# A trunk layer's opening: one block of modulation sums ahead of the first products, and K stretches in halves of the column sets

## The chip, the cores and the metric

The kernel runs on one core of one Trainium2 chip. The metric is the device time of a whole execution in microseconds (us). Five engines are named as the profile names them: PE (TensorE) multiplies, PEld loads its weights, DVE (VectorE) and ACT (ScalarE) work on tiles in on-chip memory, POOL does little here, and SP issues the transfers (DMA) from the chip's main memory. Each engine takes its instructions in the order in which they stand in its queue.

## What is computed

One decoder layer on 256 tokens of width 2048: a SwiGLU feed-forward, a mixer (pooling and windowed attention), a second feed-forward. Each is preceded by a norm and a modulation whose shift and scale come from a product of silu(c) with a 2048 x 18432 matrix, w_ada. Only the first feed-forward's start is touched:

```
mod = (silu(c) @ w_ada + b_ada).reshape(B, 9, 1, D)
h = modulate(rms_norm(x, g_ffn1), mod[:, 0], mod[:, 1])     # h * (1 + scale) + shift
x = x + 0.5 * mod[:, 2] * swiglu(h, w_ffn1_gu, w_ffn1_down) # (silu(h @ gate) * (h @ up)) @ down
```

All is float32. A product of activations and weights is made of three products of rounded halves: hi*hi, lo*hi and hi*lo.

## The kernel before

The 2048 channels are 16 ktiles of 128, and the 256 tokens two token tiles. Weight columns are taken in sets of 1024 (`Set`). For each pair of ktiles of a set, one transfer of 1 MB brings the weights (L169, tile `raw`, six buffers). For each ktile ACT casts the high half (`wh`, L180, three buffers), DVE subtracts for the low half (`wl`, L184, three buffers), and PE runs twelve products of 128 x 512 (L194, L196, L198): two token tiles, two halves of the columns, three products each. They add up in four of the eight PSUM banks. The next set takes the other four, which serve small things until then.

The opening is everything up to the end of the first six sets (gate and up columns, alternating). Their products cannot start before x is normed and the first shift and scale are known, and these need 2 x 2048 columns of w_ada, 32 MB. So the columns come in blocks (`ada_block`). A block of 256 channels brings 4 MB, for 16 ktiles of c, in rows of 1 KB; one of 512 channels brings 8 MB in rows of 2 KB. DVE multiplies each ktile's slice by c and adds it to `acc` (L450, L452). In the two 256 blocks every other ktile goes through PE instead, with c as the stationary side (L448). A product with ones sums the partitions (L456). `mod_col` turns that row, which lies alike on all partitions, into a column for each 128 channels: DVE masks with the identity (L103), reduces (L106), and adds bias and gain (L110 to L113). Then `h_mod` modulates the transposed, normed x, and writes the halves `hh` and `hl`.

The order of the work: block 0 (256 channels), then for the first set its first two ktiles, then block 1 (256 channels), and then the rest. All six sets run over four ktiles at a time (n = 0 to 3, 12 pairs of ktiles each). At the end of each such segment four banks are taken out: for n = 0 ACT copies them to on-chip memory (L520), later DVE adds them to what lies there (L522). Under n = 0, 1 and 2 the next 512-channel block is loaded and summed, one eighth (1 MB) with each pair of ktiles, `nxt.pop(0)()`, eight in twelve pairs. A scheduler orders each engine's queue from this text, so that some instructions stand ahead of others that come first in it. Transfers go to one queue, SP's, and take turns on eight completion counters: a transfer that comes eight places later waits at its issue until the earlier one on its counter has landed.

## Time and profile before

| what | value |
|---|---|
| median of three runs | 2041.13 us (2040.59 to 2041.98) |
| profiled execution, from the first instruction to the last | 2041.3 us |
| busy: PE, DVE, ACT | 2008.7, 1472.2, 987.3 us |
| transfers over the span | 523.69 MB, mean 257 GB/s |
| rows of w_ada in 512 KB loads: count, time to landing | 64, 7.5 us |

The page's first part gives busy time, share of the span and instruction count by engine; its groups give the count, the busy time, the mean duration of one in ns, the idle time of the engine before them, and what ended it. A timeline row gives start and duration in us, engine, line, operation, out<-in and count; the duration of a merged row runs from the first start to the last end. A row of windows gives a stretch, its length, the busy time of PE, PEld, DVE, ACT and POOL with their instruction counts, then PE's granted clock, the transfer engines' busy share and GB/s. Engines start an instruction before the one before it has quite ended, so the distance between two starts is shorter than the duration.

### The profile page before, as it was taken

To read this page: it belongs to the slowest core of one execution; us is meant where nothing else is said; L and a number is where in the kernel's file an instruction comes from. 1 tells how busy PE (TensorE), PEld (TensorE's weight loads), DVE (VectorE), ACT (ScalarE), POOL (GpSimd) and SP (SyncE) were. 2 spreads that over 40 slices of the span, in tenths; PEclk is the share of its full clock that TensorE was granted. 3 is DMA by queue.
4 is the path that set the end of the run, shared out by engine and by line. 5 is a ranking of instruction groups with operands and counts; after the bars stand their busy time and mean duration, and the time that the engine had idled before them with its cause. 6 is when DMAs were issued, how large, how long until landed. Compare 5 with 4: busy or idle time off the path is not lost. (4 is left out here: it accounts for less than half of the span.)

```text
span 2041.3 us, 23823 instructions
## 1 busy us (share of the span) xinstructions
PE 2008.7 (98%) x9053; PEld 1648.5 (81%) x9053; DVE 1472.2 (72%) x1698; ACT 987.3 (48%) x1324; POOL 7.3 (0%) x17
## 2 busy tenths in 40 slices
PE   6999999999999999999999999999999999999999
PEld 4788888888788887888788887788888888888887
DVE  5799878788899956777878788755555555566645
ACT  3554454444544546546554455654443444454443
POOL 0000000000000000000000000000000000000000
PEclk9999999999999999999999999999999999999999
DMA  9988758998898855776868887455655656666762
GB/s 337 356 316 301 279 198 305 334 338 313 318 350 334 333 195 183 252 278 229 293 237 288 292 283 270 165 209 207 243 206 206 228 204 214 219 223 231 233 193 69
DMA packets 157915, 523.69 MB, mean 257 GB/s; under 512 B 9353, under 2 KB 23394, under 8 KB 157544
## 3 DMA queue, kind: packets, MB, share of 16 engines
q1 hardware_dynamic: 157800, 522.16, 72.2%
q8 instruction: 71, 1.16, 0.2%
q14 instruction: 44, 0.36, 0.0%
HBM read 520.00 MB, written 2.12 MB: 256 GB/s over the span
## 5 line engine op out<-in xcount | busy, mean ns | idle before, releaser
L180 ACT CAST wh<-raw 128x1024 fp32r<-128x1024 f32 (+2 forms) x731 | 730.9, 1003 | 949.6 <-PE bank L196 874.2
L184 DVE TENSOR_TENSOR wl<-raw,wh 128x1024 fp32r<-128x1024 f32 (+2 forms) x746 | 842.0, 1136 | 452.2 <-ACT wh L180 447.2
L194 PE MATMUL bank<-wh,hh 128*128 128x512 f32 x2072 | 654.5, 390 | 6.7 <-ACT hh L278 5.7
L198 PE MATMUL bank<-wl,hh 128*128 128x512 f32 x2072 | 651.8, 389 | 0.8 <-DVE wl L184 0.5
L196 PE MATMUL bank<-wh,hl 128*128 128x512 f32 x2072 | 652.1, 389 | 0.0
L194 PEld LDWEIGHTS bank<-wh,hh 128*128 128x128 f32 x2072 | 387.1, 188 | 88.4 <-ACT hh L278 7.8
L198 PEld LDWEIGHTS bank<-wl,hh 128*128 128x128 f32 x2072 | 389.0, 188 | 83.4 <-DVE wl L184 3.9
L196 PEld LDWEIGHTS bank<-wh,hl 128*128 128x128 f32 x2072 | 388.7, 188 | 81.5 <-DVE hl L279 1.4
L129 DVE SCALAR_TENSOR_TENSOR acc<-raw,cs,acc 128x1024 f32<-128x1024 f32 x216 | 276.4, 1279 | 41.2 <-DMA raw<-in_w_ada_dram 39.4
L198 PE MATMUL bank<-wl,sh 128*128 128x512 f32 x692 | 216.9, 390 | 1.9 <-DVE wl L184 1.9
L196 PE MATMUL bank<-wh,sl 128*128 128x512 f32 x692 | 216.6, 390 | 0.3 <-DVE sl L298 0.3
L194 PE MATMUL bank<-wh,sh 128*128 128x512 f32 x692 | 216.7, 390 | 0.0
L198 PEld LDWEIGHTS bank<-wl,sh 128*128 128x128 f32 x692 | 129.7, 188 | 29.6 <-DVE wl L184 2.8
L194 PEld LDWEIGHTS bank<-wh,sh 128*128 128x128 f32 x692 | 129.7, 188 | 28.6 <-ACT wh L180 0.6
L196 PEld LDWEIGHTS bank<-wh,sl 128*128 128x128 f32 x692 | 129.8, 188 | 27.9 <-DVE sl L298 1.0
L452 DVE SCALAR_TENSOR_TENSOR acc<-raw,cs,acc 128x1024 f32<-128x1024 f32 (+1 forms) x59 | 68.1, 1154 | 7.0 <-DMA raw<-in_w_ada_dram 6.2
L298 DVE TENSOR_TENSOR sl<-big,sh 128x512 fp32r<-128x512 f32 x88 | 60.0, 683 | 4.2 <-ACT sh L297 4.2
L297 ACT CAST sh<-big 128x512 fp32r<-128x512 f32 x88 | 54.3, 621 | 8.1 <-DVE big L652 8.1
L522 DVE TENSOR_TENSOR big<-bank,big 128x512 f32<-128x512 f32 x60 | 38.1, 682 | 1.2 <-PE bank L198 0.8
L276 ACT ACTIVATE t<-bank,mcol 128x128 f32<-128x128 f32 x90 | 35.0, 463 | 7.8 <-PE bank L264 7.1
L236 ACT ACTIVATE junk<-x_sb 128x512 bf16<-128x512 f32 x24 | 15.1, 629 | 19.9 <-DVE x_sb L322 13.8
L448 PE MATMUL bank<-raw,cs 128*128 128x256 f32 x64 | 19.4, 458 | 3.3 <-DMA raw<-in_w_ada_dram 3.3
(156 smaller groups left out, 698.2 us busy)
## 6 DMA issues: line engine op xcount, KB each, us to landing
raw<-in_w_ffn_gu_dram SPq DMA_DIRECT2D x176, 1024.0 KB, 5.0
raw<-in_w_ada_dram SPq DMA_DIRECT2D x112, 1024.0 KB, 6.4
raw<-in_w_ffn_down_dram SPq DMA_DIRECT2D x88, 1024.0 KB, 5.8
raw<-in_w_in_dram SPq DMA_DIRECT2D x48, 1024.0 KB, 5.0
raw<-in_w_ada_dram SPq DMA_DIRECT2D x64, 512.0 KB, 7.5
raw<-in_w_o_dram SPq DMA_DIRECT2D x16, 1024.0 KB, 7.1
raw<-in_w_pool_up_dram SPq DMA_DIRECT2D x8, 1024.0 KB, 6.9
raw<-in_w_attn_up_dram SPq DMA_DIRECT2D x8, 1024.0 KB, 5.6
```

Of the source, the lines that this page charges most:

```text
L129: nc.vector.scalar_tensor_tensor(out=a[0], in0=raw[:, k, :], scalar=sc, in1=a[0], op0=ALU.mult, op1=ALU.add)
L180: nc.scalar.copy(wh, raw_k)
L184: nc.vector.tensor_tensor(wl[:, e], raw_k[:, e], wh[:, e].bitcast(F32), ALU.subtract)
L194: nc.tensor.matmul(self.banks[t][i], hi[:, sl], wh[:, o], start=first, stop=False)
L196: nc.tensor.matmul(self.banks[t][i], lo[:, sl], wh[:, o], start=False, stop=False)
L198: nc.tensor.matmul(self.banks[t][i], hi[:, sl], wl[:, o], start=False, stop=last)
L276: nc.scalar.activation(h[:, f, :], src, AF.Identity, scale=g_, bias=b_)
L297: nc.scalar.copy(hi, src[:, k:k + n, :])
L298: nc.vector.tensor_tensor(lo, src[:, k:k + n, :], hi.bitcast(F32), ALU.subtract)
L448: nc.tensor.matmul(banks[j], sc.to_broadcast([P, P]), r[:, j, :], start=kk == 0, stop=False)
L452: nc.vector.scalar_tensor_tensor(out=acc[0], in0=r, scalar=sc, in1=acc[0], op0=ALU.mult, op1=ALU.add)
L522: nc.vector.tensor_tensor(a, b, a, ALU.add)
```

## The change

x is loaded first, by token tiles. The first block of w_ada (256 channels) is loaded next, in four pieces, with the gains and biases between the second piece and the third. Its even ktiles go through PE with the weights as the stationary side and c as one moving column, and its sums fall out as columns (`ada_col`); no mask is needed. All other blocks are summed on DVE alone, and end in products with one column of ones. There is no second block ahead of the products: three blocks of 256 channels (two ktiles of h each) and two of 512 (four each) go one piece with each pair of ktiles, from the first pair on (`work`, `tick`). A block's last step (`done`) makes its columns, transposes x and modulates, and stands with the first piece of the next block. Norm, transposes and modulation go by pairs of channel tiles with both token tiles together (`x_T`, `h_pair`).

The sets no longer all run over four ktiles. First all six run over ktiles 0 and 1. Then the sets fall in two groups, sets 0 to 3 and sets 4 and 5: the first runs ktiles 2-3, the second 2-5, the first 4-7, the second 6-11, the first 8-15, the second 12-15. There are 24 segments as before. The first six are copied by ACT, the others added by DVE.

Lines of the changed file are about 7 further on: L187 casts `wh`, L191 makes `wl`, L446 and L448 sum into `acc`, L567 copies, L569 adds, L477 and L542 are the products with one column, L487 and L492 norm and transpose x, L505 makes `hl`.

SP's queue at the start. Names end in buffer numbers; DMAHW0 to DMAHW7 are the eight completion counters. Before:

```order
L461 DMA x_sb<-in_x_dram 128x2x2048
L469 DMA t_3_89<-in_g_ffn_dram 16x128
L469 DMA t_3_89<-in_g_mix_dram 16x128
L469 DMA t_3_89<-in_g_ffn_dram 16x128
L469 DMA t_3_89<-in_pool_scale_dram 8x128
L472 DMA t_4_94<-in_b_ada_dram 32x128 x2
L472 DMA t_4_94<-in_b_ada_dram 32x128 [waits DMAHW0_49]
L440 DMA raw_130<-in_w_ada_dram 128x4x256 [waits DMAHW1_49]
L440 DMA raw_130<-in_w_ada_dram 128x4x256 [waits DMAHW2_49]
```

and now:

```order
L81 DMA x_sb<-in_x_dram 128x2048 x2
L440 DMA raw_90<-in_w_ada_dram 128x4x256 x2
L440 DMA raw_93<-in_w_ada_dram 128x4x256 x2
L512 DMA t_5_96<-in_g_ffn_dram 16x128
L512 DMA t_5_96<-in_g_mix_dram 16x128 [waits DMAHW0_49]
L512 DMA t_5_96<-in_g_ffn_dram 16x128 [waits DMAHW1_49]
L512 DMA t_5_96<-in_pool_scale_dram 8x128 [waits DMAHW2_49]
L515 DMA t_6_101<-in_b_ada_dram 32x128 [waits DMAHW3_49]
L515 DMA t_6_101<-in_b_ada_dram 32x128 [waits DMAHW4_49]
L515 DMA t_6_101<-in_b_ada_dram 32x128 [waits DMAHW5_49]
L440 DMA raw_105<-in_w_ada_dram 128x4x256 [waits DMAHW6_49]
L440 DMA raw_105<-in_w_ada_dram 128x4x256 [waits DMAHW7_49]
```

x and two pieces of the first block now stand ahead of the gains and biases. The third piece (raw_105) waits for counter 6, which is that of the second load of raw_93.

ACT's queue at a segment's end while ACT takes the banks out. Before, from the casts of set 1's last ktiles on:

```order
L180 CAST wh_405<-raw_403 128x1024
L180 CAST wh_421<-raw_403 128x1024
L180 CAST wh_452<-raw_450 128x1024
L520 COPY big_182<-bank_360 128x512
L520 COPY big_182<-bank_361 128x512
L520 COPY big_182<-bank_362 128x512
L520 COPY big_182<-bank_363 128x512
L180 CAST wh_468<-raw_450 128x1024
```

and now, from the first set on:

```order
L187 CAST wh_223<-raw_221 128x1024
L187 CAST wh_239<-raw_221 128x1024
L567 COPY big_215<-bank_217 128x512
L567 COPY big_215<-bank_218 128x512
L187 CAST wh_273<-raw_271 128x1024
L567 COPY big_215<-bank_219 128x512
L567 COPY big_215<-bank_220 128x512
L187 CAST wh_289<-raw_271 128x1024
L567 COPY big_215<-bank_267 128x512
```

In the first list a cast of the next set (wh_452) stands ahead of the four copies. In the second the first cast of the next set (wh_273) stands behind two copies of the banks of the set before (bank_217, bank_218); so it is at the next ends too, up to the fifth.

DVE's queue where it adds the partial sums. Before, one segment of four ktiles under n = 1:

```order
L184 TENSOR_TENSOR wl_879<-raw_860,wh_878 128x1024
L452 SCALAR_TENSOR_TENSOR acc_857<-raw_941,cs,acc_857 128x1024
L184 TENSOR_TENSOR wl_910<-raw_907,wh_909 128x1024
L452 SCALAR_TENSOR_TENSOR acc_857<-raw_941,cs,acc_857 128x1024
L522 TENSOR_TENSOR big_182<-bank_814,big_182 128x512
L522 TENSOR_TENSOR big_182<-bank_815,big_182 128x512
L522 TENSOR_TENSOR big_182<-bank_816,big_182 128x512
L522 TENSOR_TENSOR big_182<-bank_817,big_182 128x512
L184 TENSOR_TENSOR wl_926<-raw_907,wh_925 128x1024
L184 TENSOR_TENSOR wl_949<-raw_946,wh_948 128x1024
L184 TENSOR_TENSOR wl_965<-raw_946,wh_964 128x1024
L452 SCALAR_TENSOR_TENSOR acc_857<-raw_980,cs,acc_857 128x1024 x2
```

and now, the second run over two ktiles (sets 0 and 1):

```order
L448 SCALAR_TENSOR_TENSOR acc_455<-raw_572,cs,acc_455 128x512
L569 TENSOR_TENSOR big_215<-bank_534,big_215 128x512
L448 SCALAR_TENSOR_TENSOR acc_455<-raw_572,cs,acc_455 128x512
L569 TENSOR_TENSOR big_215<-bank_535,big_215 128x512
L448 SCALAR_TENSOR_TENSOR acc_455<-raw_572,cs,acc_455 128x512
L569 TENSOR_TENSOR big_215<-bank_536,big_215 128x512
L569 TENSOR_TENSOR big_215<-bank_537,big_215 128x512
L191 TENSOR_TENSOR wl_590<-raw_587,wh_589 128x1024
L191 TENSOR_TENSOR wl_606<-raw_587,wh_605 128x1024
L448 SCALAR_TENSOR_TENSOR acc_455<-raw_621,cs,acc_455 128x512 x2
L569 TENSOR_TENSOR big_215<-bank_583,big_215 128x512
L448 SCALAR_TENSOR_TENSOR acc_455<-raw_621,cs,acc_455 128x512
```

Before, four low halves (wl) and three sums (acc) stand near four additions (big<-bank). Now there are two low halves and up to four narrower sums to each four additions, and the two low halves of the next segment (wl_590, wl_606) stand behind all four additions of this one.

The diff, with removed lines (they are in the kernel printed above) cut to "...":

```diff
@@ after the load of c
+    x_sb = const.tile([P, T, D], F32, name="x_sb")
+    for t in range(T):
+        nc.sync.dma_start(x_sb[:, t, :], x[0, t * P:(t + 1) * P, :])
...
@@ in place of ada_block and what follows it
+    def ada_load(c0, w, k0):
         nk = SW // w
+        raw = t_([P, nk, 2, w], "raw", RAW)
+        for j in (1, 0):
+            nc.sync.dma_start(raw[:, :, j, :], ada_v[:, k0:k0 + nk, j * D + c0:j * D + c0 + w])
+        return raw
+    def ada_acc(acc, r, kk, first):
+        sc = cs[:, kk:kk + 1]
+        if first:
+            nc.vector.tensor_scalar_mul(acc, r, sc)
+        else:
+            nc.vector.scalar_tensor_tensor(out=acc, in0=r, scalar=sc, in1=acc, op0=ALU.mult, op1=ALU.add)
+    def ada_col(c0, w, sums):
+        k, n = c0 // P, w // P
+        m0, m1 = mcol[:, 0, k:k + n], mcol[:, 1, k:k + n]
+        nc.vector.scalar_tensor_tensor(out=m1, in0=sums[1], scalar=1.0, in1=bcol[:, KD + k:KD + k + n],
+                                       op0=ALU.add, op1=ALU.add)
+        nc.vector.tensor_tensor(m1, m1, gcol[:, k:k + n], ALU.mult)
+        nc.vector.tensor_tensor(m0, sums[0], bcol[:, k:k + n], ALU.add)
+    def ada_block(c0, w):
+        acc = []
+        nk = SW // w
         def f(k0):
...
+            raw = ada_load(c0, w, k0)
+            if k0 == 0:
+                acc.append(t_([P, 2, w], "acc", 2))
+            for kk in range(nk):
+                ada_acc(acc[0], raw[:, kk], k0 + kk, k0 + kk == 0)
+        def end():
+            n = w // P
+            b = bank((P, 2, n))
             for j in (1, 0):
...
+                for a in range(n):
+                    nc.tensor.matmul(b[:, j, a:a + 1], acc[0][:, j, a * P:(a + 1) * P], ones_f[:, 0:1],
+                                     start=True, stop=True)
+            ada_col(c0, w, (b[:, 0, :], b[:, 1, :]))
+        return [lambda k0=k0: f(k0) for k0 in range(0, KD, nk)], end
+    def x_T(k):
+        xn = t_([P, T, 2 * P], "t2", T2)
+        for t in range(T):
+            nc.vector.tensor_scalar(xn[:, t, :], x_sb[:, t, k * P:(k + 2) * P], st[:, 2, t:t + 1],
+                                    st[:, 3, t:t + 1], ALU.mult, ALU.mult)
+        b = bank((P, 2, S))
+        for f in range(2):
+            for t in range(T):
+                nc.tensor.transpose(b[:, f, t * P:(t + 1) * P], xn[:, t, f * P:(f + 1) * P], ident)
+        return b
+    def h_pair(b, k, fine=False):
+        h = t_([P, 2, S], "t2", T2)
+        for f in range(2):
+            g_, b_ = mcol[:, 1, k + f:k + f + 1], mcol[:, 0, k + f:k + f + 1]
+            nc.scalar.activation(h[:, f, :], b[:, f, :], AF.Identity, scale=g_, bias=b_)
+            if fine:
+                nc.scalar.copy(hh[:, k + f, :], h[:, f, :])
+                nc.vector.tensor_tensor(hl[:, k + f, :], h[:, f, :], hh[:, k + f, :].bitcast(F32), ALU.subtract)
+        if not fine:
+            nc.scalar.copy(hh[:, k:k + 2, :], h)
+            nc.vector.tensor_tensor(hl[:, k:k + 2, :], h, hh[:, k:k + 2, :].bitcast(F32), ALU.subtract)
+    raws = [ada_load(0, 2 * P, k0) for k0 in (0, 4)]
     grow = t_([KG, P], "t2", T2)
     for i, g in enumerate((g_ffn1, g_mix, g_ffn2, pool_scale)):
         n = g.shape[1] // P
...
     for i in range(3):
         nc.sync.dma_start(brow[2 * KD * i:2 * KD * (i + 1), :],
                           b_ada[0, 3 * i * D:(3 * i + 2) * D].rearrange("(k p) -> k p", p=P))
+    raws += [ada_load(0, 2 * P, k0) for k0 in (8, 12)]
+    for t in range(T):
+        for n in range(4):
+            sumsq(t, n)
+        rstd(t)
+    xT = x_T(0)
     for col, row in ((gcol, grow), (bcol, brow)):
         n = row.shape[0]
         b = bank((P, n))
         nc.tensor.transpose(b, row, ident[:n, :n])
         nc.vector.tensor_copy(col, b)
     psc = gcol[:, 3 * KD:]
...
+    acc = t_([P, 2, 2 * P], "acc", 2)
+    sums = [[bank_at(2 * j + a, (P, 1)) for a in range(2)] for j in range(2)]
+    for kk in range(KD):
+        r = raws[kk // 4][:, kk % 4]
+        if kk % 2 == 0:
+            for j in (1, 0):
+                for a in range(2):
+                    nc.tensor.matmul(sums[j][a], r[:, j, a * P:(a + 1) * P], cs[:, kk:kk + 1],
+                                     start=kk == 0, stop=False)
+        else:
+            ada_acc(acc, r, kk, kk == 1)
+    for j in (1, 0):
+        for a in range(2):
+            nc.tensor.matmul(sums[j][a], acc[:, j, a * P:(a + 1) * P], ones_f[:, 0:1], start=False, stop=True)
+    for a in range(2):
+        ada_col(a * P, P, (sums[0][a], sums[1][a]))
     hh, hl = new_h()
     hstat = lambda k: (hh[:, k, :], hl[:, k, :])
+    h_pair(xT, 0, True)
     actT = t_([P, KF, S], "big", 1)
     part = [actT[:, a:a + 8, :].rearrange("p a b -> p (a b)").rearrange("p (t n) -> p t n", t=T)
...
+            for a in (20, 28, 36, 12, 4)]
     part.insert(4, t_([P, T, SW], "sg", 1))
     cols = [(i // 2 * SW + i % 2 * DFF, SW) for i in range(NS)]
...
+    def segment(i, k0, k1, tick):
+        s = Set(w_ffn1_gu[0], KD, cols[i], hstat)
+        for ka in range(k0, k1, 2):
+            raw = s.load(ka, 2)
+            for k in range(2):
+                s.step(ka + k, raw[:, k, :], k0, k1)
+            tick(ka)
+        for t in range(T):
+            for c_ in range(2):
+                a = part[i][:, t, c_ * CW:(c_ + 1) * CW]
+                b = s.banks[t][c_]
+                if k0 == 0:
+                    nc.scalar.copy(a, b)
+                else:
+                    nc.vector.tensor_tensor(a, b, a, ALU.add)
+                if k1 == KD and i % 2 == 0:
+                    nc.scalar.activation(a, a, AF.Silu)
+                if k1 == KD and i % 2 == 1:
+                    g = part[i - 1][:, t, c_ * CW:(c_ + 1) * CW]
+                    nc.vector.tensor_tensor(g, a, g, ALU.mult)
+    work = []
+    for c0, w in ((2, 2), (4, 2), (6, 2), (8, 4), (12, 4)):
+        fs, end = ada_block(c0 * P, w * P)
+        if work:
+            e0 = work.pop()
+            work.append([fs[0], e0])
+            fs = fs[1:]
+        work += [[f] for f in fs]
+        def done(end=end, c0=c0, w=w):
+            end()
+            for k in range(c0, c0 + w, 2):
+                h_pair(x_T(k), k)
+        work.append(done)
+    work[-1] = [work[-1]]
+    def tick(n):
+        def go(ka):
+            for _ in range(n):
+                for f in (work.pop(0) if work else ()):
+                    f()
+        return go
+    lo_, hi_ = range(0, NS // 2 + NS // 2 % 2), range(NS // 2 + NS // 2 % 2, NS)
+    for grp, k0, k1 in ((range(NS), 0, 2), (lo_, 2, 4), (hi_, 2, 6), (lo_, 4, 8), (hi_, 6, 12), (lo_, 8, KD), (hi_, 12, KD)):
+        for i in grp:
+            segment(i, k0, k1, tick(1))
     pend = sum((store_T(part[2 * i], i * SW, SW, actT) for i in range(NS // 2)), [])
```

More of the change, by code (lines that the diff above doesn't have):

```diff
@@ L454, in f @@
-            if k0 + nk == KD:
-                for j in (1, 0):
-                    nc.tensor.matmul(banks[j], ones_f, acc[0][:, j, :], start=not shared, stop=True)
-                    mod_col(j, banks[j], c0)
-        return [lambda k0=k0: f(k0) for k0 in range(0, KD, nk)]
-    nc.sync.dma_start(x_sb, x[0].rearrange("(t p) d -> p t d", p=P))
-    KG, KB = 3 * KD + PW // P, 6 * KD
-    gcol = const.tile([P, KG], F32, name="gcol")
-    bcol = const.tile([P, KB], F32, name="bcol")
+            raw = ada_load(c0, w, k0)
@@ L479, in trunk_layer @@
     psc = gcol[:, 3 * KD:]
-    for t in range(T):
-        for n in range(4):
-            sumsq(t, n)
-        rstd(t)
-    for f in ada_block(0, 256, True):
-        f()
+    acc = t_([P, 2, 2 * P], "acc", 2)
[9 more added lines that the diff above has]
+            ada_acc(acc, r, kk, kk == 1)
```

57 lines of the change are left out of this document (3 added, 54 removed).

## The prediction

> **What bounds the kernel now.** I read the busy times first, then the products on TensorE up to the end of the opening, then VectorE there by stretches of time.
>
> ```profile
> span 2041.3 us, 23823 instructions
> PE 2008.7 (98%) x9053; PEld 1648.5 (81%) x9053; DVE 1472.2 (72%) x1698; ACT 987.3 (48%) x1324; POOL 7.3 (0%) x17
> ...
> L194 PE MATMUL bank<-wh,hh 128*128 128x512 f32 x380 | 120.1, 396 | 3.3 <-ACT hh L278 2.2 <-ACT wh L180 1.0
> L196 PE MATMUL bank<-wh,hl 128*128 128x512 f32 x379 | 119.0, 393 | 0.0
> L198 PE MATMUL bank<-wl,hh 128*128 128x512 f32 x378 | 117.8, 391 | 0.0
> ...
> 312.33 0.62 PE L196 MATMUL bank<-wh,hl 128*128 128x512 f32 x2
> ...
> 317.77 0.62 PE L196 MATMUL bank<-wh,hl 128*128 128x512 f32 x2
> ```
>
> TensorE is busy for 98% of the span, so a microsecond won or lost on it in the opening reaches the end. The middle rows count the products up to 311 us: 380 + 379 + 378 = 1137. The opening has 1152 (six sets, 16 ktiles, 12 products each). The last two rows lie 24 products apart: 5.44 us, 0.2267 us each. So the opening's products end at 311 + 15 x 0.2267 = 314.4 us. Pure products would take 1152 x 0.2267 = 261.2 us; the other 53 us are what the change can touch.
>
> ```profile
> 24.46 1.54 DVE L452 SCALAR_TENSOR_TENSOR acc<-raw,cs,acc 128x512 f32<-128x512 f32 x2 [1.43 <-DMA raw<-in_w_ada_dram]
> ...
> 31.26 0.73 PE L194 MATMUL bank<-wh,hh 128*128 128x512 f32 x2
> ...
> 44.05 0.96 PE L194 MATMUL bank<-wh,hh 128*128 128x512 f32 x3 [2.21 <-ACT hh L278]
> ...
> 49.00:109.00 60.00, 58.96 (x257) 46.72 (x255) 46.50 (x46) 34.35 (x51) 0.00 (x0) 1.00 0.93 341
> ...
> 150.00:190.00 40.00, 40.00 (x178) 32.41 (x177) 38.48 (x47) 18.34 (x24) 0.95 (x1) 1.00 0.79 287
> ...
> 231.00:312.00 81.00, 81.00 (x363) 67.09 (x362) 63.91 (x79) 42.10 (x53) 0.00 (x0) 1.00 0.57 202
> ```
>
> Some 31 us go before the first product and about 11 more in the wait for the second 256-column block (31.26 to 44.05, with few products between). In the windows the fifth figure is VectorE's busy time: 46.50 of 60 us, then 38.48 of 40, then 63.91 of 81. TensorE loses nothing beside it, but in the middle there is almost no room on VectorE. This stretch is what I price the change by.
>
> **The first product.** The loads of 1 KB rows run at this rate, and the other rows give the wait from an issue to its use:
>
> ```profile
> DMA packets 3502, 3.48 MB, mean 348 GB/s; under 512 B 107, under 2 KB 3500, under 8 KB 3502
> ...
> 8.68 8.37 SPq L440 DMA_DIRECT2D raw<-in_w_ada_dram  x8
> 8.75 0.63 ACT L236 ACTIVATE junk<-x_sb 128x512 bf16<-128x512 f32 x1 [5.78 <-DMA x_sb<-in_x_dram]
> ...
> 12.31 3.75 PE L448 MATMUL bank<-raw,cs 128*128 128x256 f32 x8 [1.92 <-DMA raw<-in_w_ada_dram]
> ```
>
> x lands at 8.7 us and the block's loads are issued only then. Now their first half (2.1 MB) stands right behind x: 2.1 / 0.348 = 6.0 us, to about 14.4. The order shows the second half waiting for the counter of the first half's last load, after the gains and biases, so the queue runs dry: from 8.68 to 12.31 it took 3.6 us to bring 0.5 MB (1.5 us), so I take 1.7 us of dead time, 6.0 us of data and 0.9 us shared with the weights behind: 23.0 us (between 22 and the 24.4 of before). Then two sums (1.54), eight passes of one column (1.2, between the transposes' and the old sums' rows below), six column operations (0.6), on ScalarE two modulations and two casts of 256 columns (1.6) and, as its order has it, the cast of the first weights only behind them (1.1): first product at 29.1 us, where it was at 31.26. The wait of 11 us for the second block goes.
>
> **VectorE behind it.** Its prices:
>
> ```profile
> L184 DVE TENSOR_TENSOR wl<-raw,wh 128x1024 fp32r<-128x1024 f32 x67 | 80.5, 1219 | 14.1 <-ACT wh L180 14.0
> L452 DVE SCALAR_TENSOR_TENSOR acc<-raw,cs,acc 128x1024 f32<-128x1024 f32 x45 | 57.6, 1280 | 0.5
> L522 DVE TENSOR_TENSOR big<-bank,big 128x512 f32<-128x512 f32 x36 | 23.0, 683 | 1.2 <-PE bank L198 0.8
> L452 DVE SCALAR_TENSOR_TENSOR acc<-raw,cs,acc 128x512 f32<-128x512 f32 x9 | 6.8, 752 | 3.6 <-DMA raw<-in_w_ada_dram 3.4
> ...
> L257 DVE TENSOR_SCALAR t<-x_sb,st 128x512 f32<-128x512 f32 x6 | 3.2, 540 | 0.0
> L283 DVE TENSOR_TENSOR hl<-t,hh 128x512 fp32r<-128x512 f32 x4 | 2.7, 685 | 0.1
> ...
> 215.90 1.28 DVE L452 SCALAR_TENSOR_TENSOR acc<-raw,cs,acc 128x1024 f32<-128x1024 f32 x1
> 217.09 1.22 DVE L184 TENSOR_TENSOR wl<-raw,wh 128x1024 fp32r<-128x1024 f32 x1
> 218.23 1.28 DVE L452 SCALAR_TENSOR_TENSOR acc<-raw,cs,acc 128x1024 f32<-128x1024 f32 x1
> ...
> 224.09 2.48 DVE L522 TENSOR_TENSOR big<-bank,big 128x512 f32<-128x512 f32 x4
> 226.48 1.22 DVE L184 TENSOR_TENSOR wl<-raw,wh 128x1024 fp32r<-128x1024 f32 x1
> ```
>
> From start to start a sum of 1024 takes 1.19, a low half 1.14, an addition of a partial sum 0.60: 0.08 under the durations. A sum of 512 is then 0.67, or 0.79 where the next adds to the same tile (two took 1.54). A pair of ktiles is 24 products, 5.44 us of TensorE, and now brings one load of modulation weights until the 28th pair. For VectorE that is 2 x 1.14 + 4 x 0.75 = 5.3 us with a 256-column block, 4.7 with 512 columns. Each segment adds four partial sums, 2.4 us, except in the first six, where ScalarE copies. So pairs 7 to 10, each a segment of its own, ask 7.7 us of VectorE for 5.44 of TensorE. In before's loaded stage 12 pairs brought eight loads, and additions came once in two pairs: 8 x 2.4 + 12 x 2.28 + 6 x 2.4 + about 5 for columns and norm = 66 us to 65 of products, which just fitted.
>
> The order gives what stands on VectorE from the first low half to the one that follows the last modulation sum (29th pair): 57 low halves 64.7 us; 48 sums of 512, 18 of them chained, 33.6; 32 of 1024, 37.4; 48 additions 28.8; five hl 3.0; ten norm scalings of 256 columns 2.8; twelve column operations 1.1. Sum 171.4 us. The old masked sums (L103, L106) are gone from it, which pays for the narrower pieces.
>
> It also waits. At the segment ends of the first six pairs ScalarE stands in line as here:
>
> ```profile
> 74.35 1.08 ACT L520 COPY big<-bank 128x512 f32<-128x512 f32 x2 [5.61 <-PE bank L198]
> ...
> 75.28 0.61 PE L198 MATMUL bank<-wl,hh 128*128 128x512 f32 x2
> 75.31 1.06 ACT L180 CAST wh<-raw 128x1024 fp32r<-128x1024 f32 x1
> ...
> 76.40 1.22 DVE L184 TENSOR_TENSOR wl<-raw,wh 128x1024 fp32r<-128x1024 f32 x1 [2.31 <-ACT wh L180]
> ...
> 76.42 0.73 PE L194 MATMUL bank<-wh,hh 128*128 128x512 f32 x2 [0.52 <-ACT wh L180]
> ```
>
> Two copies wait for the set's first token tile, the next set's first cast stands behind them, and the product starts at 76.42 where 75.28 + 2 x 0.227 would do: 0.7 to 0.8 us. Before paid this twice; now it comes at each of five ends. VectorE, with 5.3 us of work in 6.2, waits 0.95 there: four times 3.8, and 2.0 where the new block's small products stand ahead. A further 1.1 goes when the sixth set's second ktile waits for the modulated pair, 3.3 where additions or columns wait for TensorE, and 1.9 for a slow start of TensorE:
>
> ```profile
> 45.00:48.50 3.50, 3.50 (x11) 0.51 1.05 399
> 48.50:60.00 11.50, 11.50 (x52) 1.00 1.04 398
> ```
>
> After the idle 2.21 us at 44.05 the granted clock stood at 0.51 for 3.5 us: 1.7 us lost, and 1.9 at the four cold microseconds that I expect at 29. Together 12.1 us of waits (between 4, if the small products and the slow clock cost VectorE nothing, and 17).
>
> **The sum.** 29.1 + 171.4 + 12.1 = 212.6 us for that low half. TensorE then has 680 products behind it and 472 to go, 107.0 us, with 1.8 us of small products and 0.5 us of transposes ahead. For the small ones (56 passes of one column in five blocks) I take 0.12 us, near the transposes; bounds 0.11 and 0.43, by these rows:
>
> ```profile
> 29.97 1.46 PE L448 MATMUL bank<-raw,cs 128*128 128x256 f32 x6
> ...
> 28.88 1.26 PE L264 MATMUL bank<-ident,t 128*128 128x128 f32 x8 [1.69 <-DVE t L257]
> ```
>
> (six of 256 columns start 0.22 apart warm, twice that cold; eight of 128 some 0.11 to 0.14 apart.) Behind pair 29 VectorE has only 2.3 us a pair and the additions, so nothing is made up and nothing lost. The opening ends at 212.6 + 1.8 + 0.5 + 107.0 = 321.9 us against 314.4: 7.5 us later. 2041.3 + 7.5 = 2048.8; the median shown, 2041.13, lies 0.2 below the profiled execution, so I say **2049 us**, 0.4% slower. The 11 us won at the start are spent because the same VectorE work is now asked of 28 pairs instead of 32.
>
> **Rivals.** (1) Faster: the sums of modulation slip into VectorE's gaps and TensorE never waits for a low half, as in before. Place: pairs 7 to 28; it decides from VectorE waits below 0 in my sum, that is if operations cost less when queued. Then TensorE alone sets the end: 29.1 + 261.2 + 1.9 clock + 5 x 0.8 ends + 28 transposes at 0.11 (3.1) + 56 passes (6.7) = 306 us, 8.4 earlier: 2033. For it: before lost nothing at 38.48 of 40. Against it: 7.7 us in 5.44 four times in a row, with three buffers of low halves as the only store. (2) No change: the waits are 4 to 8 us instead of 12.1, or the block lands at 22: 2041 to 2045. (3) Slower still: each stop for a low half at the ends of segments (by my count seven of 2 to 3 us) drops the clock as the 2.21 us did, up to 1.7 us each where VectorE then waits on additions: half of them charged, 6 us, 2055. For it the row at 45 us; against it, stops of 0.9 us at 76 us dropped nothing. The Trainium skill, "TensorE: Matmul & The Clock Gate", section "What's actually happening", says the clock halves only after an idle window of about 3.4 us. By that rule this rival costs nothing; the row with 2.21 us disagrees in part, and the row decides.
> (4) The change doesn't do what it says: the first block lands no earlier than 24.4 us and the sum moves to 2050; this stays within the forecast's own range.
>
> **How the numbers follow.** A difference of under 0.2%, 4 us, can't be told from no change. Forecast with (4), 2046 to 2053: 0.45. Slower still: 0.20. No change: 0.21. Faster: 0.14. Thus slower 0.65, same 0.21, faster 0.14. The forecast's own range is 2045 to 2054; to hold eight in ten it takes in the no-change case and most of (3): 2036 to 2057.
>
> **What will show it.** Right: first product near 29 us; VectorE over 9 tenths busy from 65 to 210 us; TensorE waiting for wl at segment ends in pairs 8 to 28; the last modulation sum near 211 us; the opening's products ending near 322. Wrong: TensorE unbroken from 65 us on (1), a first product after 32 us or before 27, a granted clock near 0.5 in pairs 7 to 28 (3), or single-column passes above 0.3 us.

## The result, and the profile after

The changed kernel takes 2055.89 us (median of 4 runs, 2054.18 to 2057.37) where the kernel before takes 2041.56 (2040.59 to 2043.39): 0.68% slower, ratio 1.0068, 95% interval 1.0054 to 1.0082. The prediction said 2049, slower, within 2036 to 2057. The profiled executions are 2054.3 and 2041.3 us.

The opening's end first. These are the first lines of the changed kernel's page, and its groups of products up to 300 us:

```profile
span 2054.3 us, 23910 instructions
PE 2011.6 (98%) x9097; PEld 1655.9 (81%) x9097; DVE 1471.7 (72%) x1709; ACT 984.4 (48%) x1306; POOL 7.3 (0%) x17
...
L201 PE MATMUL bank<-wh,hh 128*128 128x512 f32 x346 | 110.1, 399 | 4.7 <-ACT wh L187 4.6
L203 PE MATMUL bank<-wh,hl 128*128 128x512 f32 x346 | 108.3, 394 | 0.0
L205 PE MATMUL bank<-wl,hh 128*128 128x512 f32 x345 | 108.2, 401 | 11.4 <-DVE wl L191 11.4
```

They are 1037; the opening ends at 300 + (1152 - 1037) x 0.2267 = 326.1 us. The same count of the kernel before gives 1088 and 314.5. So 11.6 us arise in the opening. (VectorE's last low half of the opening agrees: it starts at 324.21 us, before at 312.71.) The last group has 11.4 us of idle TensorE ahead of it, in waits for low halves; before, it had none. The start, then the whole stretch of loads:

```profile
24.63 1.54 DVE L448 SCALAR_TENSOR_TENSOR acc<-raw,cs,acc 128x512 f32<-128x512 f32 x2 [3.22 <-DMA raw<-in_w_ada_dram]
...
26.49 1.85 PE L542 MATMUL bank<-ones_f,acc 128*128 128x1 f32 x8
30.94 0.79 PE L201 MATMUL bank<-wh,hh 128*128 128x512 f32 x1 [2.60 <-ACT wh L187]
...
30.92:216.96 186.04, 171.94 (x746) 137.00 (x747) 172.96 (x213) 79.03 (x97) 0.96 (x1) 0.98 0.92 327
76.00:84.00 8.00, 5.91 (x23) 4.47 (x22) 7.49 (x10) 2.11 (x2) 0.00 (x0) 0.88 0.99 329
84.00:92.00 8.00, 8.00 (x40) 6.66 (x39) 7.47 (x14) 2.10 (x2) 0.00 (x0) 0.91 0.85 287
100.00:112.00 12.00, 11.57 (x52) 9.16 (x51) 12.00 (x17) 4.21 (x4) 0.00 (x0) 1.00 0.86 290
124.00:136.00 12.00, 9.89 (x37) 7.76 (x36) 11.90 (x14) 3.23 (x4) 0.00 (x0) 0.86 0.96 356
```

The first block lands no earlier than before (24.63 against 24.46) and the first product gains 0.3 us. From the first low half to the end of the 29th pair's (216.96) VectorE is busy for 172.96 of 186.04 us, in parts without a gap, while TensorE idles. That looked like the forecast fulfilled. The experiments show a second bound right behind this one.

### The profile page after: what moved, and what is told of

Its sections match the earlier page's. It is cut to its first block, busy times and chain, and to the rows that moved or that the text cites. A ratio compares the mean times of both kernels' runs of the same rounds, so it can differ in the third digit from the quotient of the medians.

```text
span 2054.3 us, 23910 instructions
## 1 busy us (share of the span) xinstructions
PE 2011.6 (98%) x9097; PEld 1655.9 (81%) x9097; DVE 1471.7 (72%) x1709; ACT 984.4 (48%) x1306; POOL 7.3 (0%) x17
## 5 line engine op out<-in xcount | busy, mean ns | idle before, releaser
L187 ACT CAST wh<-raw 128x1024 fp32r<-128x1024 f32 (+2 forms) x731 | 731.3, 1003 | 948.2 <-PE bank L203 866.2
L191 DVE TENSOR_TENSOR wl<-raw,wh 128x1024 fp32r<-128x1024 f32 (+2 forms) x746 | 842.6, 1137 | 468.2 <-ACT wh L187 464.6
L205 PE MATMUL bank<-wl,hh 128*128 128x512 f32 x2072 | 652.0, 390 | 13.1 <-DVE wl L191 12.9
L205 PEld LDWEIGHTS bank<-wl,sh 128*128 128x128 f32 x692 | 130.2, 189 | 30.9 <-DVE wl L191 3.9
L448 DVE SCALAR_TENSOR_TENSOR acc<-raw,cs,acc 128x512 f32<-128x512 f32 (+1 forms) x82 | 77.0, 939 | 4.1 <-DMA raw<-in_w_ada_dram 3.2
L569 DVE TENSOR_TENSOR big<-bank,big 128x512 f32<-128x512 f32 x60 | 38.4, 681 | 3.0 <-PE bank L205 2.7
L283 ACT ACTIVATE t<-bank,mcol 128x128 f32<-128x128 f32 x60 | 23.3, 462 | 5.4 <-PE bank L271 5.4
L389 ACT COPY big<-bank 128x512 f32<-128x512 f32 x44 | 22.4, 609 | 0.1
```

The lines of the kernel that those rows point to most:

```text
L187: nc.scalar.copy(wh, raw_k)
L191: nc.vector.tensor_tensor(wl[:, e], raw_k[:, e], wh[:, e].bitcast(F32), ALU.subtract)
L205: nc.tensor.matmul(self.banks[t][i], hi[:, sl], wl[:, o], start=False, stop=last)
L283: nc.scalar.activation(h[:, f, :], src, AF.Identity, scale=g_, bias=b_)
L389: nc.scalar.copy(actT[:, k:k + 2, :].rearrange("p a b -> p (a b)"), b)
L448: nc.vector.scalar_tensor_tensor(out=acc, in0=r, scalar=sc, in1=acc, op0=ALU.mult, op1=ALU.add)
```

## The experiments

All medians and opening ends in one place; the names are explained below. The end is counted as above, from the products by 300 us of one profiled execution. The last column is what TensorE lost there to a halved clock: 1 less the granted clock, summed over stretches of 4 us from 29 to 229 us. It comes in steps of 1.7 us, one for each drop. The median of the kernel before, run beside each of the experiments, was 2042.0 to 2042.8.

| kernel | median, us | products by 300 us | opening's end, us | lost to the clock, us |
|---|---|---|---|---|
| before | 2041.6 | 1088 | 314.5 | 1.7 |
| the change | 2055.9 | 1037 | 326.1 | 3.4 |
| thin sums | 2053.7 | 1053 | 322.4 | 3.4 |
| thin additions | 2050.6 | 1072 | 318.1 | 0 |
| copies written later | 2056.0 | 1039 | 325.6 | 3.4 |
| sums shared with GpSimd | 2062.1 | 1015 | 331.1 | 5.1 |
| additions written later | 2055.5 | 1049 | 323.4 | 1.7 |
| the same, thin sums | 2051.0 | 1059 | 321.1 | 3.4 |
| the same, even stretches | 2058.5 | 1024 | 329.0 | 5.1 |
| first block in one piece | 2054.2 | 1053 | 322.4 | 0 |
| additions bound later | 2052.7 | 1052 | 322.7 | 0 |
| all orders bound | 2049.1 | 1071 | 318.4 | 0 |
| all bound, thin sums | 2037.0 | 1123 | 306.6 | 0 |
| all bound, paced | 2044.4 | 1092 | 313.6 | 0 |

**Is VectorE's load the cause?** Its work was lightened in two ways, in the sums and in the additions. These kernels leave work out to price it: thin sums add only the first ktile of each load, thin additions only one bank of four in the first 12 segments that add.

```diff
-            for kk in range(nk):
+            for kk in range(1):
                 ada_acc(acc[0], raw[:, kk], k0 + kk, k0 + kk == 0)
```

> The changed kernel, but of each load of modulation weights behind the first block VectorE sums only the first ktile (L446/L448); the others are loaded and left out of the sum. 36 of 48 sums of 512 and 16 of 32 sums of 1024 go, about 36 x 0.69 + 16 x 1.19 = 44 us of VectorE's 186 between the first low half and the last block's. Theory (VectorE's queue sets the end of the opening): TensorE's own work becomes the bound; with a first product at 30.9 us the opening ends at about 308 us, where it ended near 326; 2038 us, 2034 to 2043. Rival A (transfers: 28 pairs ask 59 MB, and the page shows 296 to 337 GB/s in the first 200 us): nothing moves, 2052 to 2057. Rival B (the late first product, the slow clock and the waits for ScalarE make the difference): 2050 or more, since none of them is touched except up to 3.4 us of clock.

```diff
-                else:
+                elif k1 == KD or (t == 1 and c_ == 1):
                     nc.vector.tensor_tensor(a, b, a, ALU.add)
```

> The changed kernel, but in the 12 segments that add partial sums before ktiles 8 to 15 are reached only one of four banks is added to its place (L569); the other three are left out. 36 additions go, 36 x 0.60 = 21.6 us of VectorE. Theory: the end moves nearly as if 21.6 us of modulation sums had gone, 12 to 18 us earlier, 2038 to 2044; the stops of TensorE at the ends of segments (82, 97, 130, 155, 183 us) go with them. Rival (the modulation loads, not the additions, hold the low halves up): 2 to 5 us, 2051 to 2054.

Thin sums: 2053.67 us (ratio to before 1.0058, 1.0037 to 1.0080). Load can't be the whole cause: 44 us less work on VectorE won 3.7 us of the opening, with the same loss to the clock. Thin additions: 2050.64 (1.0039, 1.0025 to 1.0054), where 21.6 us less work won 8.0, of which 3.4 are the clock. So a microsecond of additions weighs more than one of sums (4.6 of 21.6 against 3.7 of 44). VectorE's rows in the thin sums show why, and TensorE's waits with them:

```profile
140.71 1.28 DVE L448 SCALAR_TENSOR_TENSOR acc<-raw,cs,acc 128x1024 f32<-128x1024 f32 x1
144.29 2.65 DVE L569 TENSOR_TENSOR big<-bank,big 128x512 f32<-128x512 f32 x4 [2.29 <-PE bank L205]
146.85 2.35 DVE L191 TENSOR_TENSOR wl<-raw,wh 128x1024 fp32r<-128x1024 f32 x2
...
PE bank L205 <- DVE wl L191: 5.2, 8, 1.3
```

VectorE stands idle for 2.29 us, because the next instruction in its queue is an addition, and that waits for the segment's last products. Then come four additions, and only then the next segment's low halves, whose products are due already: TensorE stops for 0.70 us at 148.12, although VectorE had time to spare. The waits for low halves fall from 11.4 to 5.2 us and no further.

**Is it the order?** Two kernels wrote the waiting work later in the text: ScalarE's copies behind the next segment's first step, and VectorE's additions two and two behind its two steps.

```diff
+                while late:
+                    nc.scalar.copy(*late.pop(0))
...
-                    nc.scalar.copy(a, b)
+                    late.append((a, b))
```

> The changed kernel, but at the ends of the first six segments ScalarE's copies of the banks stand behind the first step of the next segment instead of ahead of it. Nothing is left out. Theory: TensorE's starts at these five ends, 0.82 to 0.95 us apart, go back to about 0.57, some 1.7 us in all, and since VectorE is the bound from pair 7 on, most of it is lost again: 2054 to 2056. Rival (these ends delay VectorE's low halves by 0.95 to 2 us each and set its start into pair 7): 2049 to 2052.

```diff
+                for _ in range(2):
+                    if late:
+                        late.pop(0)()
...
+                if k0 == 0 or k1 == KD:
+                    out()
+                else:
+                    late.append(out)
```

> The changed kernel, but a segment's four additions of partial sums (L569) are written behind the next segment's first and second low half, two and two, instead of ahead of both; the same operations, nothing left out. The thinned sums had moved the end by only 3.5 us, and their trace shows VectorE idle for 2 us ahead of four additions and the next segment's low half behind these. Theory N (the additions at the head of VectorE's queue wait for a segment's last products and then keep the next segment's low halves back by 2.4 us or more, whatever VectorE's load; its load is a second bound right below): the stops at segment ends go, VectorE's sum of 171.4 us stays with nearly no waits, the opening ends 5 to 9 us earlier than the change's 325.9: 317 to 321, 2047 to 2051. Theory V (load alone): VectorE does the same work, 0 to 3 us, 2053 to 2056.

> As the kernel with later additions, and of each modulation load behind the first block only the first ktile is summed (the others are loaded and left out), as in the thinned sums. Theory N: with the queue's order mended and the load lowered by 44 us TensorE's own work is the bound: 30.8 + 261.2 + about 10 of small products and transposes + 1.6 of slow start + 5 x 0.35 + 2 = 307 to 311 us for the opening's end, 2037 to 2042, some 12 us under the thinned sums alone. Transfers as the bound: no better than the thinned sums, 2051 to 2055.

2055.98, 2055.53 and 2051.04 us. The first is no test: the scheduler put ScalarE's queue in the same order as the change's, so it is the change once more, 0.1 us from it. In the other two it moved some of the additions and left others. In the third's trace:

```profile
144.79 2.65 DVE L575 TENSOR_TENSOR big<-bank,big 128x512 f32<-128x512 f32 x4 [2.29 <-PE bank L205]
147.36 2.35 DVE L191 TENSOR_TENSOR wl<-raw,wh 128x1024 fp32r<-128x1024 f32 x2
```

The same 2.29 us of idle VectorE, and the same order behind it. So these misses say nothing against the order. The next kernels bind it: the additions must be issued behind the low half of the next segment's second ktile. The second of them binds the copies behind its cast too, and loads the gains and biases behind the first block ("all orders" in the table). The third thins the sums as well.

```diff
+            if late:
+                with tc.issue_after(last['sub']), tc.issue_after(last['cast']):
+                    while late:
+                        late.pop(0)()
```

> The changed kernel with the order bound where writing the additions later had moved few of them: VectorE's four additions of a segment (L569) must stand behind both low halves of the next segment's first two ktiles, in every segment from the seventh on. Nothing is left out. In the change TensorE waits 12.9 us for low halves behind its first product, 4.0 go to a half clock, 8.6 to small products. Theory N (additions ahead of low halves in VectorE's queue cause the stops): 8 to 10 of the 12.9 us go and 1 to 2 of the clock, opening's end near 316, 2045 to 2048. Theory V (VectorE's load causes them, and the order only says where they show): at most 3 to 6 us, opening's end 320 to 323, 2050 to 2054.

> As the kernel with the additions bound behind the low halves, and in the first six segments ScalarE's copies (L567) too are bound behind the next segment's first two casts; gains and biases are loaded behind the first block. Nothing is left out. Theory N: of the change's 34 us beside full products the small ones (8.6), the additions' few waits (3), clock 2 and some 5 more are left; with a first product at 30.8 us the opening ends at 310 to 312, 2038 to 2043. Theory V: VectorE's 171 us from 31 us on keep it at 317 or later, 2046 to 2051.

> As the kernel with both orders bound and the gains behind, and of each modulation load behind the first block only the first ktile summed (the others are loaded and left out): 44 us less for VectorE. If the order alone caused the stops: the same as with all sums, within 2 us, 2037 to 2042. If VectorE's load is a bound of its own beside it: 5 us or more under the kernel with all sums. If the transfers bound both: both at 2046 or above.

2052.73 (1.0046, 1.0031 to 1.0061), 2049.06 (1.0032, 1.0021 to 1.0042) and 2037.04 us (0.9969, 0.9956 to 0.9982). Against the change, the additions' order won 3.4 us of the opening, all orders 7.7, thin sums 3.7, and all orders with thin sums 19.5. All but the thin sums alone are free of the change's 3.4 us of clock. Without it, binding the additions wins nothing, all orders 4.3, thin sums 3.7 and both 16.1. (Whether its shorter stops, at most 1.5 us, spared the additions bound later those drops is open.) So the first two of these kernels came out where their expectations put the theory of load alone, which the thin sums contradict, and only both together free TensorE. As the change stands, VectorE's load binds; the order is a second bound right below it, and whoever takes away one meets the other. Here are stretches of all orders bound, then of the same with thin sums, and the waits of TensorE in the latter up to 300 us:

```profile
124.00:150.00 26.00, 25.34 (x111) 20.31 (x110) 26.00 (x29) 8.99 (x9) 0.00 (x0) 1.00 0.89 325
180.00:210.00 30.00, 29.29 (x126) 23.59 (x127) 29.96 (x31) 11.21 (x11) 0.00 (x0) 1.00 0.96 362
```

```profile
124.00:150.00 26.00, 26.00 (x117) 21.52 (x116) 24.06 (x28) 9.95 (x10) 0.00 (x0) 1.00 1.03 392
180.00:210.00 30.00, 30.00 (x146) 25.11 (x145) 21.04 (x27) 13.72 (x16) 0.96 (x1) 1.00 0.87 335
...
PE bank L203 <- ACT wh L189: 3.4, 1, 3.4
PE bank L207 <- DVE wl L193: 0.5, 1, 0.5
```

With the order bound VectorE has no gap left (26.00 of 26) and TensorE still stops: this is the load. With both, TensorE runs through; its one wait for ScalarE is that ahead of the first product. The same bytes go through the queue at up to 392 GB/s, so the transfers, which several expectations named, bound neither. The copies at the first ends show in the products around 38 us, in the change and with all orders bound:

```profile
37.63 0.61 PE L205 MATMUL bank<-wl,hh 128*128 128x512 f32 x2
38.76 0.73 PE L201 MATMUL bank<-wh,hh 128*128 128x512 f32 x2 [0.52 <-ACT wh L187]
```

```profile
37.70 0.61 PE L207 MATMUL bank<-wl,hh 128*128 128x512 f32 x2
38.16 0.62 PE L203 MATMUL bank<-wh,hh 128*128 128x512 f32 x2
```

A stop of 0.7 us (from 37.63 + 2 x 0.2267 = 38.08 to 38.76) is gone.

**Other engines and other stretches.** GpSimd, nearly idle in the opening, was given a share of the sums, and the six sets were run alike.

```diff
+        if helped:
+            nc.scalar.activation(r, r, AF.Copy, scale=sc)
+            nc.gpsimd.tensor_tensor(acc, r, acc, ALU.add)
```

> The changed kernel, but the last ktile of each load behind the first block is scaled by ScalarE and added to the sum by GpSimd, which is idle there, instead of by one operation of VectorE. Nothing is left out. 12 sums of 512 and 16 of 1024 go from VectorE, 12 x 0.71 + 16 x 1.19 = 27.6 us; ScalarE gets about 24 us, in a stretch where it is busy for about half. Theory (VectorE's queue is the bound): 10 to 18 us earlier than the change, 2038 to 2046. Rival (what VectorE gives up comes back as waits, since ScalarE's casts stand behind the scalings or GpSimd is slower than 5 us for an addition): 2052 to 2065.

2062.05 us (1.0103, 1.0082 to 1.0124), slower than the change. VectorE's low halves in the change, in a row of groups from 30.9 to 217 us, and then with GpSimd, with a place of its timeline and one row of TensorE's waits:

```profile
L191 DVE TENSOR_TENSOR wl<-raw,wh 128x1024 fp32r<-128x1024 f32 x58 | 69.6, 1215 | 6.4 <-ACT wh L187 6.3
L569 DVE TENSOR_TENSOR big<-bank,big 128x512 f32<-128x512 f32 x40 | 25.8, 682 | 3.0 <-PE bank L205 2.7
```

```profile
L191 DVE TENSOR_TENSOR wl<-raw,wh 128x1024 fp32r<-128x1024 f32 x56 | 80.5, 1467 | 9.8 <-ACT wh L187 9.8
L572 DVE TENSOR_TENSOR big<-bank,big 128x512 f32<-128x512 f32 x37 | 23.7, 684 | 3.9 <-PE bank L205 3.5
...
145.68 4.56 DVE L191 TENSOR_TENSOR wl<-raw,wh 128x1024 fp32r<-128x1024 f32 x2
145.89 3.26 POOL L447 TENSOR_TENSOR acc<-raw,acc 128x1024 f32<-128x1024 f32 x1 [5.76 <-DVE acc L451]
...
PE bank L480 <- POOL acc L447: 3.8, 3, 1.6
```

A low half went from 1215 to 1467 ns on the mean, and two of them beside one addition of GpSimd took 4.56 us instead of 2.35. That takes back half of the 27.6 us given away (56 x 0.25 = 14). The 5.0 us by which the opening ends later are made up otherwise: TensorE waits 3.8 us for GpSimd's last sums, and 1.7 more go to the clock. The additions out of PSUM kept their 0.68 us, though 28 of 45 ran beside GpSimd. The Trainium skill, "SBUF — State Buffer", section "Who interferes with whom", says that a VectorE instruction with two inputs in SBUF contends with a GpSimd instruction that reads SBUF; by that rule low halves suffer and additions from PSUM do not, and both rows agree.

```diff
-... (range(NS), 0, 2), (lo_, 2, 4), (hi_, 2, 6), (lo_, 4, 8), (hi_, 6, 12), (lo_, 8, KD), (hi_, 12, KD)
+... (range(NS), 0, 2), (range(NS), 2, 6), (range(NS), 6, 12), (range(NS), 12, KD)
...
-            segment(i, k0, k1, tick(1))
+            segment(i, k0, k1, tick(2 if k0 == 0 and i >= NS - 2 else 1))
```

> As the kernel with later additions, and the six sets run K stretches of 2, 4, 6 and 4 ktiles all alike instead of in two groups; the fifth and sixth pair bring two modulation loads each. By the 27th pair VectorE then has 32 additions behind it instead of 48, and the sum from the first low half to the last block's is about 157 us, to 141 us of products. Theory N: against the kernel with later additions 3 to 6 us less, opening's end 313 to 316, 2042 to 2046. If the grouping in halves costs nothing by itself: the same as with later additions alone, or later by the 1 to 4 us that the doubled loads in pairs 5 and 6 take.

2058.49 us (1.0080, 1.0065 to 1.0095): a miss by 12. It stands on additions written later, whose order was not bound. TensorE now stops ahead of the sixth set:

```profile
69.31 0.73 PE L201 MATMUL bank<-wh,hh 128*128 128x512 f32 x2 [3.01 <-ACT wh L187]
...
84.00:150.00 66.00, 61.15 (x264) 47.43 (x262) 64.35 (x76) 23.37 (x24) 0.00 (x0) 1.00 0.92 331
```

The cast that this product waits for stands behind four copies and the modulated pair in ScalarE's queue. In additions written later it stood between the copies, and there was no stop at that place. VectorE is full again (64.35 of 66). Of the 5.6 us by which the opening ends later than there, 3.4 are the clock, and the rest is less than this stop; what the grouping in halves costs by itself stays open.

**The first block.**

```diff
-    raws = [ada_load(0, 2 * P, k0) for k0 in (0, 4)]
+    raws = [ada_load(0, 2 * P, k0) for k0 in (0, 4, 8, 12)]
...
-    raws += [ada_load(0, 2 * P, k0) for k0 in (8, 12)]
```

> The changed kernel, but the gains and biases are loaded behind all four pieces of the first modulation block instead of between the second and the third, so that the third piece no longer waits for the second to land. The last piece should land at 21.5 to 22.5 us instead of 24.6, and the first product come at 28.5 to 29.3 instead of 30.9. If what follows is a queue of work that starts with it: 1.5 to 2.5 us earlier, 2053 to 2054.5. If the first block's time is hidden by the loads behind it: 2055 to 2057.

2054.24 us (1.0063, 1.0047 to 1.0080), and 3.7 us of the opening, but not in the way expected:

```profile
17.81 6.33 PE L535 MATMUL bank<-cs,raw 128*128 128x1 f32 x29
...
20.94 0.75 DVE L448 SCALAR_TENSOR_TENSOR acc<-raw,cs,acc 128x512 f32<-128x512 f32 x1 [1.63 <-DMA raw<-in_w_ada_dram]
...
27.46 0.26 DVE L526 COPY bcol<-bank 128x96 f32<-128x96 f32 x1 [1.84 <-PE bank L525]
...
30.81 0.80 PE L201 MATMUL bank<-wh,hh 128*128 128x512 f32 x1 [3.38 <-ACT wh L187]
...
76.00:84.00 8.00, 5.91 (x26) 4.57 (x25) 7.96 (x12) 2.27 (x3) 0.00 (x0) 1.00 0.97 325
124.00:136.00 12.00, 9.90 (x44) 7.85 (x43) 12.00 (x12) 4.05 (x4) 0.00 (x0) 1.00 0.96 350
...
PE bank L205 <- DVE wl L191: 11.4, 8, 2.7
```

The block lands 3.7 us earlier, but the first product stays at 30.81. TensorE is next in line: it works at the block's one-column products until 24.1 us and then at the last passes and the transposes, so that the biases' columns come at 27.46. The waits for low halves are the change's, 11.4 us. What is gone is the half clock behind two of them (1.00 where the change has 0.88 and 0.86), 3.4 of the 3.7 us. The last section shows that the same stops can come with drops or without, so this gain can't be credited to the edit. The medians are 1.7 us apart, and the two kernels' times overlap.

**The work spread out, with nothing left out.** The loads come in more pairs than before, the sets run in another order, and ScalarE takes 2.8 us of scaling from VectorE.

```diff
+            if k == 0:
+                nc.vector.tensor_tensor(st[:, 4, t:t + 1], st[:, 2, t:t + 1], st[:, 3, t:t + 1], ALU.mult)
+            nc.scalar.activation(xn[:, t, :], x_sb[:, t, k * P:(k + 2) * P], AF.Copy, scale=st[:, 4, t:t + 1])
...
+            pairs[0] += 1
+            for _ in range(0 if pairs[0] in (16, 20, 25, 27, 30, 33) else n):
...
+    for grp, k0, k1 in ((range(5), 0, 2), ((5,), 0, 4), (range(4), 2, 4), ((4,), 2, 6), ((5,), 4, 8), (range(4), 4, 8),
+                        ((4,), 6, 12), ((5,), 8, 12), (range(4), 8, 12), (range(4), 12, KD), ((4, 5), 12, KD)):
```

> As the kernel with both orders bound and the gains behind, nothing left out, but VectorE's same work is spread over more pairs: the 28 modulation loads behind the first block come in 35 pairs instead of 28 (none with pairs 16, 20, 25, 27, 30 and 33), the six sets run in the order 0 to 4 over ktiles 0-1, set 5 over 0-3, 0 to 3 over 2-3, set 4 over 2-5, set 5 over 4-7, 0 to 3 over 4-7, set 4 over 6-11, set 5 over 8-11, 0 to 3 over 8-11, and all over the rest, and ScalarE scales x for the norm from the second pair of channel tiles on (ten operations of VectorE, 2.8 us). The three runs before it say: thin sums without the order 2053.7, the order without thin sums 2049.1, both 2037.0. Theory N with V (order and VectorE's load in pairs 7 to 28 are two bounds, one right below the other): pairs 5 to 15 ask about 66 us of VectorE to 63 of TensorE, pairs 16 to 24 about 49 to 51, so the opening ends at 308 to 313, against 318.4 with the order alone and 306.8 with thin sums: 2038 to 2044. Rival (only the total of VectorE's work, or the transfers, count): as with the order alone, 2047 to 2051.

2044.36 us over 11 runs (1.0009, 0.9997 to 1.0020): no different from the kernel before, 4.7 us under all orders bound, the opening ending at 313.6. Both lie just above what was expected. The three alterations came together, so no run shows what spreading the loads is worth alone. TensorE's waits up to 320 us:

```profile
PE bank L203 <- ACT wh L189: 4.8, 2, 4.2
PE bank L207 <- DVE wl L193: 3.8, 5, 1.2
```

No version with all its work beat the kernel before. The 306.6 us of all bound with thin sums are what this opening takes where TensorE hardly waits behind its first product.

## Why the prediction was right, and what it did not see

Direction and engine were right, and so was the forecast's reason, VectorE's work. A second bound that it did not see lay a few microseconds below, where it didn't touch the sum. For the first product, here are two stretches of the changed kernel's transfers (TensorE's busy time, its clock, the transfer engines' share, GB/s):

```profile
14.00:16.00 2.00, 2.00 (x11) 1.00 0.23 42
16.20:24.60 8.40, 7.45 (x35) 1.00 1.02 353
```

- **First product, 29.1 us: 30.94.** The block was put at 23.0, the last sums began at 24.63; rival (4) had 24.4. The dead time of the queue was sized about rightly: 1.7 us, and the row from 14 to 16 shows 1.8 lost. The term that was too small is the time shared with the weights behind, 0.9: from 16.2 to 24.6 the queue moved 3.0 MB, of which 2.1 are the block's, so some 2.5 us went to others. Behind the block 6.1 us were worked out and 6.3 measured, with the eight cold passes at 1.85 instead of 1.2. And the block's landing was not worth what the sum gave it: with it at 20.94 the first product came at 30.81.
- **VectorE's 171.4 us: 172.96. Its waits, 12.1: 13.1** (186.04 - 172.96). The signs named for it (9 tenths busy, stops for low halves at segment ends) were all there. Low half at 212.6, measured 216.96, of which 1.8 are the first product's.
- **The first segment ends, 0.7 to 0.8 us each at five of them: 0.7** (38.08 to 38.76).
- **From the 29th pair's low half 109.3 us (107.0, 1.8 and 0.5): 109.1** to 326.1. The opening's end was 321.9 in the forecast, 4.2 early.
- **Rival (3), clock.** The sum charged 1.9 us at the start; rival (3) named drops behind the stops and gave them 6. In the change the rows from 76 to 84 and 124 to 136 us (0.88, 0.86), with 84 to 92 at 0.91, make 1.0 + 1.7 + 0.7 = 3.4 us. With the same stops and no drop the opening ended at 322.4, close to the forecast's 321.9. So the forecast missed the opening's end mostly by what that execution lost to the clock.
- **"The 11 us are spent because the same VectorE work is now asked of 28 pairs instead of 32".** This holds as far as it goes: binding the additions alone, with all the work kept, leaves the end where it was but for the clock. What the sum did not see is that VectorE's queue is not a sack of work with waits added to it. The order rows of the change, four additions ahead of the next two low halves, stood beside it and got only a share of 3.3 us, for VectorE's own waits. By the row at 144.29 such an end holds the low half back by a wait and 2.6 us of additions, whatever else VectorE does. That this left the sum alone is luck: without the clock the order alone ends the opening at 319.0 (thin sums), the change's load at 322.7.
- **Rival (1), 306 us and 2033:** 306.6 and 2037.0, once both bounds were off and 44 us of sums left out. Its condition (VectorE's gaps suffice) needed the order as well. Its total was right, with terms that shifted against each other: the first product came 1.8 us later than in it, and the 4.0 for the first segment ends were gone with the copies' order. The kernel before has a low half of the next segment ahead of its additions and no wait for one.
- **The rest.** The medians differ by 14.3 us, the openings by 11.6, so some 3 us seem to lie behind the opening: all thirteen kernels with the changed opening have a median 1729.5 to 1732.5 us above their opening's end, the kernel before 1727.1. But a median and an opening's end come from different executions. Within the profiled ones the rest takes 1726.8 us before, 1728.2 in the change and 1725.6 to 1734.3 in all thirteen. No run settles where these 3 come from.

## What to carry to other kernels

When an engine looks full beside a stalled one, read the row ahead of the stall before adding up its work: an instruction that waits for the stalled engine, queued ahead of what that engine needs next, makes both look busy. Test order and load crosswise, since two bounds a few microseconds apart hide each other, and each alone looks harmless. And look at the queue that a scheduler made of an edit before reading its time: text that is written later may not be issued later.

## What was not expected of the hardware

The clock behind a stop is not a matter of the stop's length alone. In the change a half clock follows stops of 2.09 and 2.11 us, but not one of 2.68 us, as TensorE's timeline and the stretches behind the three stops show:

```profile
81.11 1.26 PE L205 MATMUL bank<-wl,hh 128*128 128x512 f32 x4 [2.09 <-DVE wl L191]
129.86 1.65 PE L205 MATMUL bank<-wl,hh 128*128 128x512 f32 x3 [2.11 <-DVE wl L191]
182.82 1.20 PE L205 MATMUL bank<-wl,hh 128*128 128x512 f32 x4 [2.68 <-DVE wl L191]
...
82.00:86.00 4.00, 4.00 (x12) 3.10 (x11) 3.07 (x6) 0.19 (x1) 0.00 (x0) 0.57 0.93 278
130.00:134.00 4.00, 4.00 (x11) 3.23 (x12) 4.00 (x4) 0.94 (x1) 0.00 (x0) 0.59 1.00 356
183.00:187.00 4.00, 4.00 (x18) 3.29 (x19) 4.00 (x4) 1.52 (x2) 0.00 (x0) 1.00 0.67 230
```

The kernel with its copies written later has the change's order on VectorE and ScalarE, instruction for instruction. Its stops are the same (2.09, 1.69, 2.11, 1.51 and 2.70 us), but there the clock fell behind the first and the last, and not behind the 2.11 us at 129.67:

```profile
181.01 2.08 PE L205 MATMUL bank<-wl,hh 128*128 128x512 f32 x4 [2.70 <-DVE wl L191]
...
130.00:134.00 4.00, 4.00 (x19) 3.27 (x18) 4.00 (x4) 1.49 (x2) 0.00 (x0) 1.00 0.98 347
181.00:185.00 4.00, 3.99 (x12) 3.20 (x13) 4.00 (x4) 1.04 (x1) 0.00 (x0) 0.63 0.62 202
```

With the first block in one piece the same waits (11.4 us, the longest again 2.7) brought no drop at all. And a drop needs no long stop: in thin sums the clock stood at 0.53 from 212 to 215 us, behind sixteen products of one column and a wait of 0.56 us ahead of them (209.32). So a profiled execution of this kernel carries up to 3.4 us that its stops only make possible. Whoever compares two traces that differ by so little should compare their clocks first. The Trainium skill, "TensorE: Matmul & The Clock Gate", section "What's actually happening", has a free-running window of about 3.4 us, and a halved clock after an idle one. That the drop depends on where a stop falls fits these rows; that the window must be idle does not, since the longest stop that it followed lasted 2.7 us.
